# First scale as whole-fp32 products, one VectorE instruction for each other modulation unit, one square in the MLP

## The chip, the core and the metric

One core of a Trainium2 chip runs the program. The metric is the device time of one execution in microseconds (us). Its engines work side by side and wait for each other through semaphores: PE (TensorE, matrix products), DVE (VectorE), ACT (ScalarE), POOL (GpSimd) and SP, which here only issues DMAs, in the order of its queue. Each engine works through its own instructions in order.

## What is computed

Two blocks on 256 tokens of 1024 features, in fp32: eight stages in a row. The first block's two layers have a modulation that comes from one vector `c`:

```python
c_act = silu(c)
for i in range(2):
    mod = c_act @ ada_w[i] + ada_b[i]            # [1024] @ [1024, 6144]
    sh1, sc1, gt1, sh2, sc2, gt2 = split(mod, 6)
    h = rmsnorm(x, norm_g[i, 0]) * (1 + sc1) + sh1
    y = short_conv(h) if i == 0 else rwkv7(h)    # conv: h @ w_in [1024, 3072], ..., @ w_out
    x = x + gt1 * y
    h = rmsnorm(x, norm_g[i, 1]) * (1 + sc2) + sh2
    x = x + gt2 * (square(relu(h @ mlp_w1[i])) @ mlp_w2[i])   # 1024 -> 4096 -> 1024
# second block: sparse attention, MLP, decaying attention, MLP, each MLP again square(relu(.))
```

## The kernel before

Features lie on the 128 partitions (eight tiles `kt` of 128), tokens on the free axis. All large weights come as one stream of units of 128 x 1024 fp32 (512 KB; a DMA `raw` on SP brings two, 1 MB, into one of two buffers). A unit is one tile of 128 outputs against 1024 inputs. `_split` makes two fp32r parts of it: ACT copies the unit into `H` (L350) and DVE subtracts to get `L` (L352). The operand is split too (`zh`, `zl`). `mm3` then takes three products for each kt: H zh, H zl, L zh (L383 to L385), 24 products for a unit. Splits run three units ahead of the products. The stages in order, with their units: conv 32, mlp0 64, rwkv 34, mlp1 64, dsa 25, mlp2 64, fox 32, mlp3 64.

An MLP runs in two halves: 16 up units, then 16 down units (8 output tiles of two units). An up tile is evacuated as `mt` (times `rstd`, DVE L733), `mr` (relu, ACT), `hh` (square on ACT, L739), `ma` (square again on DVE, L741), `hlo` (`ma` - `hh`, DVE L744).

**The modulation.** `ada_w` has 96 units of 128 outputs x 1024 inputs, outputs on the partitions. A unit is loaded into a tile `adu` (13 buffers, SP queue; in rwkv 24 of them come as `raw`) and reduced against `cact`, a copy of silu(c) on every partition, in one of two ways: on DVE by a multiply-and-reduce (L539), or by a product on POOL (L544) followed by a summing copy on ACT (L547). The trace has 53 of the first and 43 of the second kind. Each is followed on DVE by an addition of the bias to 128 x 1 numbers (L553), and for the two scales of a layer by g (1 + scale) (L558), column by column. `ada_plan` loads a unit six stream units before it is used and multiplies on POOL two units (`PLEAD`) before the ACT sum.

**The start.** SP issues `cols`, `cact`, the input `x` in two halves, then modulation units of part (0, 0) (first scale) and (0, 1) (first shift) mixed with `raw` pairs. The squares of x are summed tile by tile on DVE into `acc`, and two products with a column of ones give the sums of a token. `conv_start` walks over kt: scale unit and shift unit of kt, then `z0` = x times rstd, `z`, `zh`, `zl`; the first six conv tiles, split in spaces of their own (`hls`, `hy`), take their products with tile kt as soon as it is there. All six finish together after kt = 7.

The order on each engine is not written by hand: a planner orders the program's instructions by priority (program order, shifted for splits and norms) and by its own costs.

The parts of the first two stages are told apart below by the start of their last evacuation: six conv tiles at 63.3 us, the 18 others at 133.4, eight output tiles at 158.1, six first mlp0 tiles at 181.3, ten more up tiles at 218.2, 16 down units at 272.4, 16 up units at 316.4, 16 down units at 361.6.

Of the kernel before, what the change touches and what calls it, by code (L numbers as in the profile page):

```python
# [29 lines left out]
PLEAD = 2  # L30
# [5 lines left out]
SHP = [1, 0, 0, 0, 0, 1, 0, 1]  # L36
# [10 lines left out]
CSL = [2, 2]  # L47
CSP = 5
CSK = [1, 2, 3, 4]
# [67 lines left out]
def rwkv_units(I):  # L117
# [4 lines left out]
    # the output product in two halves of its input, two tiles of 128 outputs in a unit  # L122
# [4 lines left out]
def rwkv_consts():  # L127
    """masks of the chunked recurrence; rows are (head of the pair, step j)"""
# [44 lines left out]
def att_consts():  # L173
    """rotary tables (rows: dims of two heads) and the causal masks"""
# [9 lines left out]
def stage_units(stage, I):  # L184
# [11 lines left out]
    if stage == "mlp2" or stage == "mlp3":  # L196
# [6 lines left out]
        ("kk", 8), ("ka", 8), ("rk", 8), ("lnw", 8), ("lnb", 8), ("gaa", 8), ("gkv", 8), ("gab", 8), ("bf", 1)]  # L203
# [7 lines left out]
# order of the modulation parts (shift, scale, gate, ...) as they are needed  # L211
# [3 lines left out]
def layout(I, stages):  # L215
# [4 lines left out]
    if len(units) % 2:  # L220
# [4 lines left out]
    ad = I["ada_w"].reshape(2, D, 6, 8, 128)[:, :, MODORD].transpose(0, 2, 3, 4, 1)  # L225
    a["ada"] = ad.reshape(48, 2, 128, D).transpose(0, 2, 1, 3)
# [9 lines left out]
        "bf": np.concatenate([I["b_f_2"], np.zeros(112, np.float32)])[:, None],  # L236
    }
# [12 lines left out]
# ---------------------------------------------------------------- the program  # L250

class Prog:
# [3 lines left out]
    def __init__(s, ctx, tc, d, out):  # L256
# [19 lines left out]
        nc.sync.dma_start(s.cols, d["cols"])  # L276
# [11 lines left out]
    def phase(s, ada, early=False):  # L288
        """the space of modulation weights"""
# [34 lines left out]
    # ---- the weight stream  # L324

    def _dma(s):
        p = s.dma_to
        s.R[p] = s.raw.tile([128, 2, D], F32, name="raw")
        n, i = s.pairs[p]
        s.nc.sync.dma_start(s.R[p], s.d[n][i])  # L330
        s.dma_to += 1

    def _split(s):
# [5 lines left out]
        if s.pairs[p][0] == "ada":  # L339
            return  # L340
# [22 lines left out]
    def ada_raw(s):  # L363
        """a unit of the stream that is a modulation's; False if a product's unit comes next"""
# [4 lines left out]
        s.ada_one(s.R[u // 2][:, u % 2], i, POOLRAW[i % len(POOLRAW)])  # L369
# [8 lines left out]
    # ---- matrix products, weights stationary  # L378
# [29 lines left out]
    def rows_gen(s, n, z, evac):  # L408
        """z (its parts) times n times 256 columns, tokens in the rows; evac(m, psums of the halves of the tokens)"""
# [34 lines left out]
    def pump(s, until):  # L444
        """issue steps of what was spawned"""
# [23 lines left out]
    def norm_shift(s, shift):  # L469
        """shift: [128, 8], a column more for the products"""  # L470
# [16 lines left out]
    def token_sums(s, ps, *accs):  # L487
        """for each accumulator, two columns of the sums over the features"""
# [27 lines left out]
    # ---- modulation of the first block  # L516

    def ada_setup(s):
# [3 lines left out]
        nc.scalar.activation(s.cact, s.cact, AF.Silu)  # L522
        s.mod = s.const.tile([128, 2, 6, 8], F32, name="mod")
# [4 lines left out]
    def ada_load(s, i):  # L528
        """unit i: (layer, part in MODORD, tile of 128 outputs)"""
# [54 lines left out]
    def conv_start(s):  # L584
        """the first norm and the first eight tiles of the convolution's products, as the modulation's weights come in"""
        nc = s.nc
        s.new_z()
        hl = [s.big.tile([128, 2, 2, KT, 128], F32R, name=f"hls{i}", tag=f"h{i}") for i in range(2)]
        hy = [s.big.tile([128, 2, KT, 128], F32R, name=f"hy{i}", tag=f"y{'hl'[i]}") for i in range(2)]
        s.hlx = dict(enumerate([hl[0][:, 0], hl[0][:, 1], hl[1][:, 0], hl[1][:, 1], hy[0], hy[1]][:GN]))  # L590
# [8 lines left out]
        for kt in range(KT):  # L599
            s.sq_feed(kt)  # L600
# [1165 lines left out]
```

## Time and profile before

| | |
|---|---|
| median of 3 runs | 1479.45 us (1477.5 to 1485.63) |
| profiled execution, span from its first to its last instruction | 1478.3 us (no time of its own around the span is given; the median lies 1.15 us above it) |
| PE busy | 1347.5 us, 91% |
| DVE busy | 1116.8 us, 76% |
| ACT busy | 774.6 us, 52% |
| POOL busy | 287.6 us, 19% |

In a list of groups each row has line, engine, operation, output <- inputs, shapes and count, then busy us, mean ns of one, and idle time before. In a timeline a row has start us, duration us, then the same names. In a table of windows a row has the stretch, its length, and for each engine the busy us and the number of instructions, then the granted PE clock (share of full), the DMA share and GB/s. Busy PE counts matmuls until their modelled end, so a stretch with waits can still read nearly full.

### The profile page before, as it was taken

How to read it: one execution, taken by the hardware profiler on the slowest of the kernel's cores; microseconds unless marked ns; L12 is line 12 of the kernel's file. 1: busy time of each engine (PE TensorE's matmuls, PEld its weight loads, DVE VectorE, ACT ScalarE, POOL GpSimd, SP SyncE). 2: the span in 40 equal slices, each digit the busy share in tenths (PEclk: the TensorE clock that was granted, in tenths of full speed). 3: DMA queues.
4: the chain of work that ended last, by engine and by line, in shares of the span. 5: the costliest groups of instructions: out<-in, count | busy, mean ns of one | idle time of the engine just before them, and what ended most of it. 6: DMA issues, size and time to landing. Idle time of an engine off the chain costs nothing.

```text
span 1478.3 us, 26839 instructions
## 1 busy us (share of the span) xinstructions
PE 1347.5 (91%) x10616; PEld 1295.6 (88%) x10616; DVE 1116.8 (76%) x2146; ACT 774.6 (52%) x1443; POOL 287.6 (19%) x224
## 2 busy tenths in 40 slices
PE   1879899998988877998999998899999999999997
PEld 1879889998778877888999987699999998999997
DVE  6889899775998998569758768877566749676665
ACT  3645574553666642226536644755355547564553
POOL 5141432102585462122000043200000000000000
PEclk9999999999889988799999999999999999999999
DMA  7577777655024553134555543246555463355553
GB/s 304 210 288 260 257 282 284 215 183 203 30 100 147 173 193 119 40 127 166 200 192 179 187 164 125 90 153 204 193 178 194 159 241 115 115 199 176 196 176 111
DMA packets 46621, 263.43 MB, mean 178 GB/s; under 512 B 5440, under 2 KB 9744, under 8 KB 20512
## 3 DMA queue, kind: packets, MB, share of 16 engines
q1 hardware_dynamic: 46288, 261.13, 50.5%
q8 instruction: 84, 1.38, 0.4%
q0 software_dynamic: 208, 0.59, 0.1%
q14 instruction: 41, 0.34, 0.1%
HBM read 257.69 MB, written 2.11 MB: 176 GB/s over the span
## 4 chain that ended last, share of the span: by engine, by line
PE 65%; DVE 21%; DMA 4%; POOL 4%; ACT 4%; issue 2%; SPq 0%; POOLq 0%; DVEq 0%; ACTq 0%
PE mm L384 18%; PE mm L383 18%; PE mm L385 18%; DVE HL L352 5%; DMA adu<-in_ada_dram 2%; DVE mod L553 2%; DVE adu L539 1%; DMA raw<-in_w_dram 1%; ACT HL L350 1%; DVE raw L539 1%; POOL adu L544 1%; PE ax L845 1%; PE mm L419 1%; PE ax L419 1%; PE ax L838 1%
## 5 line engine op out<-in xcount | busy, mean ns | idle before, releaser
L352 DVE TENSOR_TENSOR HL<-raw,HL 128x1024 fp32r<-128x1024 f32 x372 | 470.9, 1271 | 176.6 <-ACT HL L350 176.1
L350 ACT ACTIVATE HL<-raw 128x1024 fp32r<-128x1024 f32 x372 | 389.1, 1056 | 290.4 <-PE mm L385 237.2
L383 PE MATMUL mm<-zh,HL 128*128 128x256 f32 (+1 forms) x1328 | 381.9, 288 | 15.5 <-DVE mt L733 4.1
L385 PE MATMUL mm<-zh,HL 128*128 128x256 f32 (+1 forms) x1328 | 380.5, 287 | 8.8 <-DVE HL L352 8.8
L384 PE MATMUL mm<-zl,HL 128*128 128x256 f32 (+1 forms) x1328 | 379.7, 286 | 1.1 <-DVE zl L719 1.1
L384 PE MATMUL mm<-hlo,HL 128*128 128x256 f32 x1024 | 287.9, 281 | 0.0
L385 PE MATMUL mm<-hh,HL 128*128 128x256 f32 x1024 | 287.7, 281 | 0.0
L383 PE MATMUL mm<-hh,HL 128*128 128x256 f32 x1024 | 285.0, 278 | 0.0
L383 PEld LDWEIGHTS mm<-zh,HL 128*128 128x128 f32 x1328 | 255.9, 193 | 20.4 <-issue 10.5
L385 PEld LDWEIGHTS mm<-zh,HL 128*128 128x128 f32 x1328 | 256.5, 193 | 10.4 <-DVE HL L352 10.4
L384 PEld LDWEIGHTS mm<-zl,HL 128*128 128x128 f32 x1328 | 257.1, 194 | 1.4 <-DVE zl L719 1.3
L383 PEld LDWEIGHTS mm<-hh,HL 128*128 128x128 f32 x1024 | 193.3, 189 | 0.0
L384 PEld LDWEIGHTS mm<-hlo,HL 128*128 128x128 f32 x1024 | 192.5, 188 | 0.0
L385 PEld LDWEIGHTS mm<-hh,HL 128*128 128x128 f32 x1024 | 192.3, 188 | 0.0
L544 POOL TENSOR_TENSOR adu<-adu,cact 128x1024 f32<-128x1024 f32 x35 | 97.5, 2788 | 176.7 <-DMA adu<-in_ada_dram 174.6
L507 POOL TENSOR_TENSOR r<-r,mhalf 128x2 f32<-128x2 f32 x6 | 7.3, 1210 | 529.1 <-DVE r L502 529.1
L383 PE MATMUL mm<-yh,HL 128*128 128x256 f32 x272 | 81.0, 300 | 8.8 <-DVE x L1626 4.0
L384 PE MATMUL mm<-yl,HL 128*128 128x256 f32 x272 | 80.0, 295 | 0.0
L385 PE MATMUL mm<-yh,HL 128*128 128x256 f32 x272 | 79.1, 292 | 0.3 <-DVE HL L352 0.3
L741 DVE TENSOR_TENSOR ma<-mr 128x256 f32<-128x256 f32 x128 | 57.4, 455 | 17.2 <-ACT mr L736 16.6
L383 PEld LDWEIGHTS mm<-yh,HL 128*128 128x128 f32 x272 | 53.4, 198 | 10.8 <-ACT yh L1193 4.6
L736 ACT ACTIVATE mr<-mm 128x256 f32<-128x256 f32 x64 | 24.3, 383 | 69.9 <-PE mm L385 69.9
(454 smaller groups left out, 2460.5 us busy)
## 6 DMA issues: line engine op xcount, KB each, us to landing
raw<-in_w_dram SPq DMA_DIRECT2D x190, 1024.0 KB, 4.9
adu<-in_ada_dram SPq DMA_DIRECT2D x72, 512.0 KB, 7.4
raw<-in_ada_dram SPq DMA_DIRECT2D x12, 1024.0 KB, 5.1
cb<-cd SPq DMA_DIRECT2D x1, 2048.0 KB, 9.4
rs<-raw SPq DMA_DIRECT2D x28, 64.0 KB, 1.9
x<-in_x_dram SPq DMA_DIRECT2D x2, 512.0 KB, 6.7
R<-in_wa_dram SPq DMA_DIRECT2D x2, 512.0 KB, 6.8
bvd<-bv SPq DMA_DIRECT2D x8, 128.0 KB, 4.8
```

Source lines behind the costliest of these rows:

```text
L350: s.nc.scalar.activation(h, raw, AF.Copy)
L352: s.nc.vector.tensor_tensor(l, raw, h.bitcast(F32), op=OP.subtract)
L383: mm(ps, H[:, kt], rh, start=start, stop=False)
L384: mm(ps, H[:, kt], rl, start=False, stop=False)
L385: mm(ps, L[:, kt], rh, start=False, stop=stop)
L419: s.nc.tensor.matmul(ps[j][:, :256], a, b[:, k], start=kt == i == 0, stop=kt == 7 and i == 2)
L539: s.nc.vector.tensor_tensor_reduce(t, t, s.cact, scale=1.0, scalar=0.0, op0=OP.mult, op1=OP.add, accum_out=s.modf[:, i:i + 1])
L544: s.nc.gpsimd.tensor_tensor(t, t, s.cact, op=OP.mult)
L553: V.tensor_tensor(m, m, s.c("adab", i), op=OP.add)
L736: nc.scalar.activation(r, ps[:, :T], AF.Relu)
L741: nc.vector.tensor_tensor(a, r, r, op=OP.mult)
L838: tr(pt[:, 128 * j:128 * j + 128], lg[e][:, 128 * j:128 * j + 128], s.ident)
```

## The change

The first scale's eight units are stored with inputs on the partitions and multiplied on PE (eight fp32 products of one column each against `ccol`, silu(c) as columns); the result, still in PSUM, goes with the bias plus one (`a1`) into `gp` in one DVE instruction. The first six conv tiles are multiplied unsplit, in fp32: weights straight from `raw` (three pairs in spaces of their own), the operand `z` kept whole in `zf` beside its split. All other modulation units (88) are one DVE multiply-and-reduce whose starting value is the bias; POOL and ACT have no part in them, and the 128 x 1 additions are gone; g (1 + scale) is taken once for eight columns, after the eighth unit. x is loaded first on SP, in four parts, `cols` on ACT's queue; the squares of x go to PE unsummed (16 products with the column of ones in place of seven DVE additions and two). In the MLP ACT takes the square once in fp32 (`ma`) and copies it to `hh`; DVE only subtracts.

```diff
-CSL = [2, 2]
-CSP = 5
-CSK = [1, 2, 3, 4]
+ADAPE = range(8)
+CSP = 4
+CSW = [1, 3, 5]
-    def ada_one(s, t, i, pool=False):
-        if pool:
-            s.ada_mul(t)          # POOL
-            s.ada_sum(t, i)       # ACT, then ada_end on DVE
-        else:
-            s.nc.vector.tensor_tensor_reduce(t, t, s.cact, scale=1.0, scalar=0.0, op0=OP.mult, op1=OP.add,
-                                             accum_out=s.modf[:, i:i + 1])
-            s.ada_end(i)
+    def ada_one(s, t, i):
+        s.nc.vector.tensor_tensor_reduce(t, t, s.cact, scale=1.0, scalar=s.c("adab", i), op0=OP.mult, op1=OP.add,
+                                         accum_out=s.modf[:, i:i + 1])
         q, part = i % 8, i // 8 % 6
-        if part in (0, 3):
-            V.scalar_tensor_tensor(s.gpf[:, k:k + 1], m, 1.0, s.c("ng", k), op0=OP.add, op1=OP.mult)
+        if q == 7 and part in (0, 3):
+            s.nc.vector.scalar_tensor_tensor(s.gpf[:, k:k + 8], s.modf[:, i - 7:i + 1], 1.0, s.c("ng", k, 8), ...)
+    def ada_pe(s, t, ps):
+        w = t.rearrange("p (k m) -> p k m", k=KT)
+        for k in range(KT):
+            s.nc.tensor.matmul(ps, w[:, k], s.ccol[:, k:k + 1], start=k == 0, stop=k == KT - 1)
     # _split
+        if u < s.whole:
+            s.H[u], s.L[u] = s.R[p][:, u % 2].rearrange("p (k m) -> p k m", k=KT), None
+            return
     # ada_plan
-            if POOLADA[k % len(POOLADA)]:
-                at(max(u0, u - PLEAD), lambda i=i: s.ada_mul(tiles[i]))
-                at(u, lambda i=i: s.ada_sum(tiles.pop(i), i))
-            else:
-                at(u, lambda i=i: s.ada_one(tiles.pop(i), i))
+            at(u, lambda i=i: s.ada_one(tiles.pop(i), i))
     # conv_start, for each kt
+            pm = s.axbank()
+            s.ada_pe(st[kt][0], pm[:, :1])
+            s.ada_one(st[kt][1], 8 + kt)
+            loads(kt + CSP + 1)
+            V.scalar_tensor_tensor(g, pm[:, :1], a1[:, kt:kt + 1], s.c("ng", kt), op0=OP.add, op1=OP.mult)
+            V.tensor_tensor(t, s.x[:, kt], s.rstd[:, :T], op=OP.mult)
+            A.activation(z, t, AF.Identity, bias=s.mod[:, 0, 1, kt:kt + 1], scale=g)      # z = zf[:, kt]
+            A.activation(s.zh[:, kt, :T], z, AF.Copy)
+            V.tensor_tensor(s.zl[:, kt, :T], z, s.zh[:, kt, :T].bitcast(F32), op=OP.subtract)
-                    s.mm3(tiles[i][:, :T], w, k, s.zh[:, k, :T], s.zl[:, k, :T], k == 0, k == KT - 1)
+                    mm(tiles[i][:, :T], w[:, k], zf[:, k], start=k == 0, stop=k == KT - 1)
     # mlp, up
-            nc.scalar.activation(s.hh[:, m], r, AF.Square)
             a = s.t("ma")
-            nc.vector.tensor_tensor(a, r, r, op=OP.mult)
+            nc.scalar.activation(a, r, AF.Square)
+            nc.scalar.activation(s.hh[:, m], a, AF.Copy)
```

## Rows read from the trace of the kernel before

**Rows 1.** Page, part 1: the span.

```profile
span 1478.3 us, 26839 instructions
```

**Rows 2.** Windows of the start, of conv and mlp0 by part, and of rwkv's middle and end.

```profile
0.00:31.00 31.00, 3.29 (x10) 2.22 (x10) 17.85 (x29) 12.91 (x23) 16.41 (x12) 1.00 0.94 362
31.00:63.30 32.30, 23.59 (x139) 21.60 (x140) 26.27 (x49) 17.35 (x31) 6.16 (x3) 0.89 0.40 148
63.30:133.40 70.10, 60.14 (x448) 57.76 (x447) 63.22 (x109) 35.30 (x58) 26.21 (x9) 0.93 0.71 263
133.40:158.10 24.70, 23.12 (x191) 22.54 (x189) 23.83 (x43) 15.81 (x29) 2.40 (x1) 1.00 0.88 307
158.10:181.30 23.20, 19.34 (x141) 18.57 (x142) 18.95 (x33) 10.48 (x21) 12.03 (x5) 0.93 0.75 285
181.30:218.20 36.90, 32.12 (x243) 31.73 (x242) 36.38 (x65) 27.35 (x51) 10.49 (x5) 0.91 0.72 257
218.20:272.40 54.20, 51.62 (x434) 51.24 (x432) 46.14 (x67) 26.24 (x33) 17.65 (x6) 1.00 0.78 282
272.40:316.40 44.00, 43.37 (x340) 43.40 (x341) 36.29 (x65) 28.53 (x46) 0.00 (x0) 0.93 0.56 187
316.40:362.00 45.60, 45.14 (x382) 44.94 (x380) 25.39 (x34) 18.65 (x24) 0.34 (x1) 1.00 0.49 167
...
440.00:560.00 120.00, 96.95 (x758) 94.58 (x757) 110.03 (x209) 66.66 (x168) 66.47 (x50) 0.91 0.49 167
661.40:678.00 16.60, 12.60 (x94) 12.40 (x93) 15.68 (x24) 11.95 (x24) 6.52 (x3) 0.90 0.60 217
```

**Rows 3.** Timeline at 12 us: a POOL product and a DVE addition of 128 x 1.

```profile
11.85 2.62 POOL L544 TENSOR_TENSOR adu<-adu,cact 128x1024 f32<-128x1024 f32 x1 [9.90 <-DMA adu<-in_ada_dram]
12.19 2.30 DVE L553 TENSOR_TENSOR mod<-mod,cols 128x1 f32<-128x1 f32 x1
```

**Rows 4.** Groups by line and shape, whole execution.

```profile
L352 DVE TENSOR_TENSOR HL<-raw,HL 128x1024 fp32r<-128x1024 f32 x372 | 470.9, 1271 | 176.6 <-ACT HL L350 176.1
...
L544 POOL TENSOR_TENSOR adu<-adu,cact 128x1024 f32<-128x1024 f32 x35 | 97.5, 2788 | 176.7 <-DMA adu<-in_ada_dram 174.6 <-ACT yh L671 1.5
...
L741 DVE TENSOR_TENSOR ma<-mr 128x256 f32<-128x256 f32 x128 | 57.4, 455 | 17.2 <-ACT mr L736 16.6 <-ACT mr L734 0.6
...
L739 ACT ACTIVATE hh<-mr 128x256 fp32r<-128x256 f32 x128 | 52.4, 414 | 1.9
L539 DVE CUSTOM_DVE_ANT_0 adu<-adu,cact 128x1024 f32<-128x1024 f32 x37 | 47.2, 1275 | 0.0
...
L553 DVE TENSOR_TENSOR mod<-mod,cols 128x1 f32<-128x1 f32 x96 | 36.4, 396 | 4.6 <-ACT adu L547 4.1
```

**Rows 5.** Groups of DVE from 63.3 to 133.4 us.

```profile
L352 DVE TENSOR_TENSOR HL<-raw,HL 128x1024 fp32r<-128x1024 f32 x19 | 24.8, 1333 | 0.8 <-ACT HL L350 0.7
L659 DVE SCALAR_TENSOR_TENSOR cvv<-u,cols,cvv 128x256 f32<-128x256 f32 x16 | 13.8, 868 | 0.7 <-ACT cvv L655 0.6
...
L553 DVE TENSOR_TENSOR mod<-mod,cols 128x1 f32<-128x1 f32 x17 | 8.4, 511 | 0.0
```

**Rows 6.** Timeline of PE: fp32 products of 256, of one and of two columns.

```profile
378.51 0.60 PE L1215 MATMUL ax<-hx,R 128*128 128x256 f32 x2
378.95 0.60 PE L1216 MATMUL ax<-hx,R 128*128 128x256 f32 x2
...
15.41 1.01 PE L491 MATMUL ax<-ones,acc 128*128 128x1 f32 x4 [15.41 <-DVE acc L778]
...
449.68 0.51 PE L1367 MATMUL ax<-rc,R 128*128 128x2 f32 x4
```

**Rows 7.** SP's timeline: issues of the third pair and of the last first-shift units.

```profile
35.99 0.33 SPq L330 DMA_DIRECT2D raw<-in_w_dram  x1
36.37 0.90 SPq L531 DMA_DIRECT2D adu<-in_ada_dram  x2
```

**Rows 8.** Chain that ended last, in order of time: one piece of mlp0.

```profile
231.20 5.64 DMA adu<-in_ada_dram
```

More of the change, by code (lines that the diff above doesn't have):

```diff
@@ L225, in layout @@
     ad = I["ada_w"].reshape(2, D, 6, 8, 128)[:, :, MODORD].transpose(0, 2, 3, 4, 1)
+    ad = ad.reshape(96, 128, D).copy()
+    for i in ADAPE:
+        ad[i] = ad[i].T.reshape(KT, 128, 128).transpose(1, 0, 2).reshape(128, D)
     a["ada"] = ad.reshape(48, 2, 128, D).transpose(0, 2, 1, 3)
@@ L236, in layout @@
         "bf": np.concatenate([I["b_f_2"], np.zeros(112, np.float32)])[:, None],
+        "cc": col(I["c"].reshape(-1)),
     }
@@ L275, in __init__ @@
         s.cols = s.const.tile([128, NCOL], F32, name="cols")
-        nc.sync.dma_start(s.cols, d["cols"])
+        nc.scalar.dma_start(s.cols, d["cols"])
         s.ident = s.const.tile([128, 128], F32, name="ident")
@@ L327, in _dma @@
         p = s.dma_to
-        s.R[p] = s.raw.tile([128, 2, D], F32, name="raw")
+        s.R[p] = s.rawx.pop(p) if p in s.rawx else s.raw.tile([128, 2, D], F32, name="raw")
         n, i = s.pairs[p]
@@ L500, in _norm_close, with _norm_factor @@
         s.token_sums(ps, s.acc)
+        return s._norm_factor(ps, squared, copy)
+    def _norm_factor(s, ps, squared=False, copy=True):
+        nc = s.nc
         r = s.wk.tile([128, 2], F32, name="r")
@@ L522, in ada_setup @@
         nc.scalar.activation(s.cact, s.cact, AF.Silu)
+        s.ccol = s.const.tile([128, KT], F32, name="ccol")
+        nc.scalar.activation(s.ccol, s.c("cc"), AF.Silu)
         s.mod = s.const.tile([128, 2, 6, 8], F32, name="mod")
@@ L586, in conv_start @@
         nc = s.nc
+        V, A, mm = nc.vector, nc.scalar, nc.tensor.matmul
         s.new_z()
-        hl = [s.big.tile([128, 2, 2, KT, 128], F32R, name=f"hls{i}", tag=f"h{i}") for i in range(2)]
-        hy = [s.big.tile([128, 2, KT, 128], F32R, name=f"hy{i}", tag=f"y{'hl'[i]}") for i in range(2)]
-        s.hlx = dict(enumerate([hl[0][:, 0], hl[0][:, 1], hl[1][:, 0], hl[1][:, 1], hy[0], hy[1]][:GN]))
+        hs = [s.big.tile([128, 2, 2, D], F32, name=f"hs{i}", tag=f"h{i}") for i in range(2)]
+        s.rawx = {p: hs[p // 2][:, p % 2] for p in range((GN + 1) // 2)}
+        s.whole = GN
+        sq = s.big.tile([128, KT, T], F32, name="sq0", tag="yh")
+        zf = s.big.tile([128, KT, T], F32, name="zf", tag="yl")
         st = []
@@ L596, in loads @@
                 st.append((s.ada_load(kt), s.ada_load(8 + kt)))
-        for i in (0, 4):
-            nc.sync.dma_start(s.x[:, i:i + 4], s.d["x"][:, i:i + 4])
-        for kt in range(KT):
-            s.sq_feed(kt)
-        s.norm_close()
-        for n in CSL:
-            loads(n)
-            s._dma()
-        loads(CSP)
-        tiles, units, at = [], [], []
-        for kt in range(KT + 1):
-            if kt < KT:
-                s.ada_mul(st[kt][1])
-                s.ada_one(st[kt][0], kt)
-            if kt:
-                j = kt - 1
-                s.ada_sum(st[j][1], 8 + j)
-                t = s.t("z0")
-                nc.vector.tensor_tensor(t, s.x[:, j], s.rstd[:, :T], op=OP.mult)
-                z = s.t("z1")
-                nc.scalar.activation(z, t, AF.Identity, bias=s.mod[:, 0, 1, j:j + 1], scale=s.gp[:, 0, j:j + 1])
-                nc.scalar.activation(s.zh[:, j, :T], z, AF.Copy)
-                nc.vector.tensor_tensor(s.zl[:, j, :T], z, s.zh[:, j, :T].bitcast(F32), op=OP.subtract)
-            loads(kt + CSP)
-            while len(units) < GN and kt >= CSK[len(units) // 2]:
-                units.append(s.unit(0))
-                tiles.append(s.mmbank() if len(tiles) < 3 else s.axbank())
@@ new lines, in loads @@
+                if kt in CSW:
+                    s._dma()
+        loads(CSP)
+        a1 = s.wk.tile([128, KT], F32, name="a1")
+        V.tensor_scalar(a1, s.c("adab", 0, KT), 1.0, None, op0=OP.add)
+        for kt in range(KT):
+            A.activation(sq[:, kt], s.x[:, kt], AF.Square)
+        ps = s.axbank()
+        for j in range(2):
+            for kt in range(KT):
+                mm(ps[:, j:j + 1], sq[:, kt, 128 * j:128 * j + 128], s.ones, start=kt == 0, stop=kt == KT - 1)
+        s._norm_factor(ps)
@@ new lines, in conv_start @@
+        tiles = [s.mmbank() if i < 3 else s.axbank() for i in range(GN)]
+        units, at = [], []
+        for kt in range(KT):
+            pm = s.axbank()
+            s.ada_pe(st[kt][0], pm[:, :1])
+            s.ada_one(st[kt][1], 8 + kt)
+            loads(kt + CSP + 1)
+            g = s.gp[:, 0, kt:kt + 1]
+            V.scalar_tensor_tensor(g, pm[:, :1], a1[:, kt:kt + 1], s.c("ng", kt), op0=OP.add, op1=OP.mult)
+            t = s.t("z0")
+            V.tensor_tensor(t, s.x[:, kt], s.rstd[:, :T], op=OP.mult)
+            z = zf[:, kt]
+            A.activation(z, t, AF.Identity, bias=s.mod[:, 0, 1, kt:kt + 1], scale=g)
+            A.activation(s.zh[:, kt, :T], z, AF.Copy)
+            V.tensor_tensor(s.zl[:, kt, :T], z, s.zh[:, kt, :T].bitcast(F32), op=OP.subtract)
+            while len(units) < GN and kt >= CSW[len(units) // 2]:
+                units.append(s.unit(0)[0])
@@ L624, in conv_start @@
                 at.append(0)
             for i, w in enumerate(units):
-                while at[i] < kt:
+                while at[i] <= kt:
                     k = at[i]
-                    s.mm3(tiles[i][:, :T], w, k, s.zh[:, k, :T], s.zl[:, k, :T], k == 0, k == KT - 1)
+                    mm(tiles[i][:, :T], w[:, k], zf[:, k], start=k == 0, stop=k == KT - 1)
                     at[i] += 1
@@ L1633, in run @@
         s.feed = lambda kt: None
-        s.hlx = {}
+        s.hlx, s.rawx, s.whole = {}, {}, 0
         s.early = next((s.start[n] for n in stages if n not in ("conv", "mlp0")), 2 * len(s.pairs))
         s.phase(ADAB if first else 0, True)
-        if stages[0] != "conv":
-            nc.scalar.dma_start(s.x, s.d["x"])
+        for i in range(0, KT, 2):
+            nc.sync.dma_start(s.x[:, i:i + 2], s.d["x"][:, i:i + 2])
         if first:
```

23 lines of the change are left out of this document (6 added, 17 removed).

## Prediction

> **What bounds the kernel now.** I read the table of windows first, cut where a part of a stage ends [rows 2]. A part whose products are never late shows PE's own pace: the last 16 units of mlp0 take 45.6 us, 2.85 us a unit, 0.119 us for each of its 24 products. The reader then holds every other part of the first two stages against that pace. The 18 conv units from 63.3 to 133.4 us need 51.3 and take 70.1 (18.8 lost); the eight of the output product need 22.8 and take 24.7 (1.9); the six first of mlp0 17.1 against 23.2 (6.1); the next ten 28.5 against 36.9 (8.4); the 16 down units 45.6 against 54.2 (8.6); the two parts after 272.4 lose nothing. So some 44 us are lost between 63.3 and 272.4, and before 63.3 us only six tiles are finished. What ends the waits is in the DVE column of the same rows: 63.2 of 70.1, 23.8 of 24.7, 36.4 of 36.9. DVE sets the pace there; in the down part (46.1 of 54.2) something else does.
>
> Why DVE is so full shows the timeline beside it [rows 3]: a DVE addition of 128 numbers of one column starts 0.34 us after a POOL product and ends with it, 2.30 us later. The same addition takes 0.396 on the mean over all 96 [rows 4]. DVE stands while POOL multiplies. In the conv part the lines on DVE are long in the same way [rows 5]: L659 868 ns, L553 511 ns, L352 1333 ns.
>
> The down part has its own cause. The chain of waits there holds the landing of a modulation unit, 5.64 us after its issue [rows 8], with the POOL product, the ACT sum and so ACT's next splits behind it; SP issues such a unit only behind a `raw` pair that waits for its buffer. The start shows the same queue [rows 7]: the third pair is issued at 35.99 us, when a first split frees its buffer, and the last two units of the first scale and shift stand behind it until 36.37, with DMA idle ahead (148 GB/s from 31 to 63.3, 362 before [rows 2]).
>
> **The change, part by part.** All sums are against the span of 1478.3 us [rows 1]; the median shown is 1.15 us above it.
>
> *Start.* The bytes up to the last first-shift unit: 16 modulation units of 0.524 MB, three pairs of 1.05, x 1.05, `cact` 0.52, `cols` 0.16, together 13.3 MB. The kernel before moved 362 x 31 = 11.2 MB in its first 31 us; at that mean rate the other 2.1 take 5.8 us, so the last unit lands near 37. No issue waits for a buffer any more: the pairs have their own space, and the 13 buffers of units are reused only after a first product. PE's work: 64 one-column products and 48 whole products. One column costs (1.01 / 4) 0.25 us in the start's rows and 0.51 / 4 = 0.13 us later [rows 6], which I take as PE's clock at its lower and its higher level. A whole product of 256 columns costs (378.95 - 378.51) / 2 = 0.22 us [rows 6], less than the three split ones, 0.36. At the lower level I double it. So PE needs 8 + 11 = 19 us at the higher and 16 + 21 = 37 at the lower level, from about 17 us (token sums at 15.41 now [rows 6]). At the higher level data sets the end: 37 plus eight one-column products (1), four small dependent steps on DVE and ACT (2, at some 0.45 each [rows 4]), six whole products (1.3): 41. At the lower, with the chain gp, z, product unhidden (0.6 us for each kt): 59. The stretch that holds the head now had a clock of 0.89 [rows 2], so I take 46, nearer to the higher level: 17 us earlier than 63.3 (4 to 22). The 16 products of squares (4 us at most) replace a sum that DVE took tile by tile; same answer either way. Six splits (1.27 us each [rows 4]) leave DVE and ACT; their gain is inside this term.
>
> *Conv, 18 units.* DVE gains what POOL's nine products [rows 2] held. Against quiet durations (1.215 for L352, 0.48 for L659, 0.15 for L553) the three lines of rows 5 are long by 2.2 + 6.2 + 6.1 = 14.5 us, 1.6 for each POOL product (at most 2.15, as in rows 3). The additions' own 17 x 0.15 = 2.6 and the eight gp columns (1.2) go too. It takes on nine reductions at 1.275 [rows 4] less overlap, 1.2: 10.8. The sum is -7.5, to 62.6 us, still above PE's 51.3. I take -8 (-4, if ACT's and DMA's waits grow; -14 if every POOL product had cost 2.15 and lines outside rows 5 shrink).
>
> *Output product and first six mlp0 tiles.* Losses 1.9 and 6.1. One and four POOL products fall away, but the second shift's eight reductions are in DVE's order just before its products, and the first norm_split waits for g (1 + scale) of all eight columns. I take -3 (0 to -6).
>
> *Next ten up tiles.* 16 times `ma` leave DVE (0.455 each, 7.3 us [rows 4]), and four or five POOL products' waits (7), for five reductions (6). DVE falls from 36.4 to about 28, PE's own 28.5. I take -7 (-4 to -8.4).
>
> *Down units.* A unit is now needed only at its own time instead of two units (5.7 us) earlier, which is what the landing missed [rows 8], and ACT's queue no longer holds a sum. But SP's order stays, and DVE, not POOL, now stands if a unit is late, and behind it the splits. I take -6 (-3 to -8.6).
>
> *rwkv.* 440 to 560 has DVE at 110 of 120 us [rows 2] and the inverse of the triangles on it. Six to eight POOL products (1.6 each, 11) and 24 additions (0.1 to 0.15 without POOL, 3) go, eight reductions (10) come: -4 on a full engine, and ACT and POOL are freer: I take -6 (+2 to -10).
>
> *End of rwkv, mlp1.* 661.4 to 678 is four units (11.4) in 16.6 us with DVE at 15.7 and three POOL products: -2.5 (0 to -5).
>
> *The square elsewhere.* From 272.4 on PE sets the pace of the MLPs [rows 2], so the DVE time of the other 112 `ma` (51 us) is cover, not gain: nothing. ACT takes 0.41 more for each tile [rows 4]: from 28.5 us in the 44 of an up part to 35, still covered by PE. That cover is gone only if a tile's ACT work passes 2.75 us.
>
> *Starting value.* A bias column in place of the constant 0.0 in the reduction shows nowhere. Nothing to some 0.07 us (L659's quiet 0.48 against 0.41 of a two-input form) for 88, at most 6 us, partly hidden; I take nothing.
>
> Sum: 17 + 8 + 3 + 7 + 6 + 6 + 2.5 = 49.5 us; 1478.3 - 49.5 = 1428.8, and with 1.15 for the median, 1430.
>
> *A rule against it.* The rows give a whole fp32 product as 0.22 us [rows 6], two split ones. The Trainium skill, FP8 and Floating Point Precision, TensorE Precision Notes, counts four passes through the array for true FP32. By it 48 whole products would take some 23 us at the higher level instead of 11. The trace disagrees, with its 0.22 beside it; it is a rival below.
>
> **Rivals.**
> DVE stays the bound: 35 more reductions land on an engine with 63 of 70 us busy, and DMA bursts keep waits as they are. Then only the start, half of the up part and 1 or 2 elsewhere remain, some 22 us: 1457. For it: DVE needs 62 us where PE needs 51; against it: rows 3. Chance 0.15.
> The start runs at the lower clock: 59 instead of 46, 1443. For it: 64 products of one column in a thin stream, 0.25 us each at 15 us; against it: the products between them. Chance 0.12.
> Whole products cost as much again in this place, 0.44 at the higher level, if the pair that rows 6 time is no measure of 48: 48 x 0.22 = 10.6 us of PE work more, all of it on the start's end: 1440. Against it, each of the rows' two pairs gives 0.22. Chance 0.03. (This is where the rule of the Trainium skill's FP8 and Floating Point Precision would lead.)
> All that was lost comes back, PE bound from 42 us on: 21 + 18 + 8 + 8 + 8 + 10 = 73: 1406. Chance 0.09.
> The change does not free DVE: if its long instructions were long for another reason, it gains 17 + 5 and pays 25 reductions of 1.2 less the additions in the same parts: 1473 to 1483. Rows 3 say otherwise. Chance 0.03.
> Slower: ACT becomes the bound of the up parts. The copy waits for the square just ahead of it, and if that pair cost not 0.41 but 1.5 us more for a tile, the 112 tiles that PE bounds now would each lose (28.5 / 16 + 1.5 - 2.75 =) 0.53 us, 60 us in all, more than the 49.5: 1490. For it: two dependent instructions in a row; against it: 414 ns on the mean [rows 4]. Chance 0.03.
>
> **How the numbers follow.** The forecast, 1430, has 0.55 (its own range 1414 to 1446). The range 1408 to 1458 takes in the clock and the pass rivals, most of a bound DVE, and the sum's ends for all but extreme mixes. Faster by over 0.5%, about 7.4 us and what a measurement of this kernel can tell from no change: 0.55 + 0.15 + 0.12 + 0.03 + 0.09 = 0.94; within: 0.03; slower: 0.03.
>
> **What would show it.** In the windows of the changed kernel: six conv tiles done near 46 us, with DMA above 360 GB/s until 37; POOL without L544 and no DVE line above its quiet time; whole products 0.22 us apart; 18 conv units in about 62 us with DVE still full; ten up tiles near 30; down units near 48; 44 to 46 as now for the late halves of the MLPs. Wrong would be a start beyond 55 us, a conv part still at 70, or a late MLP half above 47 with ACT full.

## The result, and the profile after

The changed kernel takes 1439.14 us (median of 4 runs, 1434.7 to 1442.18) beside 1480.7 for the kernel before (4 runs in the same comparison): ratio 0.971, 95% interval 0.968 to 0.974. That is 41.6 us less, inside the range and 9 us above the forecast of 1430. The sum hides two large errors, though. The table sets the parts beside the forecast; a part ends at the start of its last evacuation, but the start and the six mlp0 tiles, which finish together, at the first (the start 62.2 us before), all from the timelines of the two profiled executions, which differ by 39.3 us at the last part's end.

| part | before | after | measured | forecast |
|---|---|---|---|---|
| start, six conv tiles | 62.2 | 62.4 | +0.2 | -17 |
| 18 conv units | 71.1 | 58.3 | -12.8 | -8 |
| output product, first six mlp0 tiles | 46.5 | 43.7 | -2.8 | -3 |
| ten up tiles | 38.6 | 34.6 | -4.0 | -7 |
| 16 down units | 54.0 | 46.2 | -7.8 | -6 |
| late half of mlp0 | 89.2 | 88.6 | -0.6 | 0 |
| rwkv | 316.2 | 303.0 | -13.2 | -6 and most of -2.5 |
| mlp1 to the end | 790.6 | 792.3 | +1.7 | rest of -2.5 |

The windows of the changed kernel, cut at these ends, answer to [rows 2]: stretch, its length, busy us and number of instructions of PE, PEld, DVE, ACT and POOL, the granted PE clock, DMA share and GB/s.

```profile
0.00:31.00 31.00, 22.57 (x108) 21.09 (x109) 8.48 (x28) 8.54 (x18) 1.61 (x6) 1.00 0.95 364
31.00:62.40 31.40, 30.48 (x143) 25.55 (x142) 10.45 (x22) 6.97 (x12) 0.00 (x0) 0.78 0.41 167
62.40:120.70 58.30, 56.02 (x452) 54.54 (x451) 55.07 (x101) 26.81 (x42) 0.00 (x0) 1.00 0.84 306
120.70:146.20 25.50, 22.78 (x193) 22.61 (x192) 23.66 (x43) 13.69 (x26) 0.00 (x0) 1.00 0.90 309
146.20:164.40 18.20, 16.40 (x131) 15.57 (x130) 16.06 (x30) 7.84 (x14) 1.68 (x1) 1.00 0.86 319
164.40:199.00 34.60, 33.35 (x277) 32.97 (x276) 32.66 (x57) 29.57 (x57) 0.00 (x0) 1.00 0.82 303
199.00:245.20 46.20, 46.09 (x389) 45.89 (x389) 40.23 (x56) 19.44 (x21) 0.00 (x0) 1.00 0.88 314
245.20:288.50 43.30, 43.30 (x363) 43.30 (x362) 32.48 (x49) 34.26 (x61) 0.00 (x0) 1.00 0.58 196
```

From 62.4 us on this is the picture that was forecast: POOL empty, DVE still full in the conv part (55.1 of 58.3), the down units near PE's own pace, the late up half unchanged with ACT at 34.3 of 43.3. The second row is not. From 31 to 62.4 us DVE is busy for a third and ACT for less, the transfers are over by 45 us, and PE is busy for 30.5 of 31.4 us. The groups of PE between 5 and 63.4 us say with what.

```profile
L630 PE MATMUL mm<-zf,hs 128*128 128x256 f32 x48 | 18.9, 549 | 2.9 <-ACT zf L621 2.7
L558 PE MATMUL ax<-ccol,adu 128*128 128x1 f32 x128 | 18.1, 275 | 0.0
L630 PE MATMUL ax<-zf,hs 128*128 128x256 f32 x44 | 11.9, 421 | 0.0
L607 PE MATMUL ax<-ones,sq 128*128 128x1 f32 x32 | 7.0, 353 | 5.5 <-ACT sq L603 5.5
```

The counts are what the reader is to see. The code issues 64 one-column products (L558) and 16 of squares (L607); the trace has 128 and 32. Six tiles of 8 whole products are 48; the trace has 48 in the `mm` banks alone and as many in the `ax` banks (44 of them by 63.4 us). One fp32 product is two instructions. What the prediction took from [rows 6] as two products 0.22 us apart was one product. How PE goes through them is in its timeline (start, duration, then the names):

```profile
13.99 6.83 PE L558 MATMUL ax<-ccol,adu 128*128 128x1 f32 x32
...
23.96 2.93 PE L630 MATMUL mm<-zf,hs 128*128 128x256 f32 x6 [1.86 <-ACT zf L621]
26.68 4.01 PE L558 MATMUL ax<-ccol,adu 128*128 128x1 f32 x32
30.55 1.74 PE L630 MATMUL mm<-zf,hs 128*128 128x256 f32 x4
33.17 5.08 PE L630 MATMUL mm<-zf,hs 128*128 128x256 f32 x12 [0.88 <-ACT zf L621]
38.09 1.89 PE L630 MATMUL ax<-zf,hs 128*128 128x256 f32 x8
39.82 3.63 PE L558 MATMUL ax<-ccol,adu 128*128 128x1 f32 x32
...
48.31 5.78 PE L630 MATMUL ax<-zf,hs 128*128 128x256 f32 x26
53.92 3.63 PE L558 MATMUL ax<-ccol,adu 128*128 128x1 f32 x32
57.41 2.16 PE L630 MATMUL mm<-zf,hs 128*128 128x256 f32 x6
```

From 26.68 us on each group starts where the one ahead ends, but for one wait of 0.88 us for `zf`: two scale units (x32), then the whole products that these two kt allow, then the next two scale units. From 53.92 to 57.41 us, 32 instructions of one column take 3.49 us, 0.109 each; from 48.31 to 53.92, 26 of 256 columns take 5.61, 0.216 each. Both stretches have a clock of 1.00, the level of 2.4 GHz. So a scale unit costs PE 16 x 0.109 = 1.7 us there, and a whole product 0.43, more than the three split ones it replaces (0.36).

Earlier the same work takes twice as long: 6.83 / 32 = 0.213 us for one column from 13.99 us on, (26.68 - 23.96) / 6 = 0.45 for 256 columns. That is the spacing of the lower level, 1.2 GHz, as in this window, whose column reads 0.50 (in the timeline its products stand 0.43 us apart):

```profile
33.00:36.00 3.00, 2.83 (x7) 2.26 (x8) 1.63 (x3) 0.54 (x2) 0.00 (x0) 0.50 1.04 415
```

The column reads 1.00 for the first 31 us all the same. Up to some 27 us here, and for longer in some of the kernels below, the spacing and the column disagree, and the level is read from the spacing.

The groups of DVE from 62.4 to 120.7 us answer to [rows 5]:

```profile
L356 DVE TENSOR_TENSOR HL<-raw,HL 128x1024 fp32r<-128x1024 f32 x19 | 22.8, 1227 | 0.3 <-ACT HL L354 0.3
L545 DVE CUSTOM_DVE_ANT_0 adu<-adu,cact,cols 128x1024 f32<-128x1024 f32 x16 | 20.2, 1287 | 0.0
L661 DVE SCALAR_TENSOR_TENSOR cvv<-u,cols,cvv 128x256 f32<-128x256 f32 x16 | 7.7, 487 | 0.6 <-ACT cvv L657 0.5
```

The split fell from 1333 to 1227 ns and L659 (now L661) from 868 to 487: in the kernel below that only takes POOL out they are at 1234 (whole execution) and 480, so POOL's part made them long.

### The profile page after: what moved, and what is told of

Its sections match the earlier page's. It is cut to its first block, busy times and chain, and to the rows that moved or that the text cites. A ratio compares the mean times of both kernels' runs of the same rounds, so it can differ in the third digit from the quotient of the medians.

```text
span 1439.8 us, 26749 instructions
## 1 busy us (share of the span) xinstructions
PE 1357.8 (94%) x10724; PEld 1303.4 (91%) x10724; DVE 1019.3 (71%) x1959; ACT 772.5 (54%) x1480; POOL 172.8 (12%) x181
## 4 chain that ended last, share of the span: by engine, by line
PE 72%; DVE 15%; DMA 4%; POOL 4%; ACT 2%; issue 2%; POOLq 0%; DVEq 0%; SPq 0%; ACTq 0%
PE mm L388 18%; PE mm L387 18%; PE mm L389 18%; DVE HL L356 4%; DMA raw<-in_w_dram 3%; DVE adu L545 2%; PE mm L630 1%; PE ax L558 1%; PE mm L423 1%; PE ax L423 1%; PE ax L847 1%; ACT HL L354 1%; PE ax L630 1%; PE ax L840 1%; POOL R L1455 1%
## 5 line engine op out<-in xcount | busy, mean ns | idle before, releaser
L356 DVE TENSOR_TENSOR HL<-raw,HL 128x1024 fp32r<-128x1024 f32 x372 | 458.1, 1238 | 229.5 <-ACT HL L354 229.0
L389 PE MATMUL mm<-zh,HL 128*128 128x256 f32 (+1 forms) x1328 | 376.1, 284 | 5.9 <-DVE HL L356 5.8
L387 PE MATMUL mm<-zh,HL 128*128 128x256 f32 (+1 forms) x1328 | 376.8, 284 | 4.4 <-DVE x L701 1.6
L388 PE MATMUL mm<-zl,HL 128*128 128x256 f32 (+1 forms) x1328 | 375.1, 283 | 0.0
L387 PEld LDWEIGHTS mm<-zh,HL 128*128 128x128 f32 x1328 | 251.3, 189 | 8.4 <-issue 3.8
L389 PEld LDWEIGHTS mm<-zh,HL 128*128 128x128 f32 x1328 | 251.5, 190 | 7.6 <-DVE HL L356 7.6
L388 PEld LDWEIGHTS mm<-zl,HL 128*128 128x128 f32 x1328 | 252.2, 190 | 0.0
L545 DVE CUSTOM_DVE_ANT_0 adu<-adu,cact,cols 128x1024 f32<-128x1024 f32 x64 | 81.2, 1280 | 2.0 <-DMA adu<-in_ada_dram 2.0
L746 DVE TENSOR_TENSOR hlo<-ma,hh 128x256 fp32r<-128x256 f32 x128 | 53.5, 421 | 5.8 <-ACT hh L743 3.1
L743 ACT ACTIVATE hh<-ma 128x256 fp32r<-128x256 f32 x128 | 52.9, 417 | 3.5
```

Of the source, the lines that this page charges most:

```text
L356: s.nc.vector.tensor_tensor(l, raw, h.bitcast(F32), op=OP.subtract)
L387: mm(ps, H[:, kt], rh, start=start, stop=False)
L388: mm(ps, H[:, kt], rl, start=False, stop=False)
L389: mm(ps, L[:, kt], rh, start=False, stop=stop)
L743: nc.scalar.activation(s.hh[:, m], a, AF.Copy)
L746: nc.vector.tensor_tensor(s.hlo[:, m], a, s.hh[:, m].bitcast(F32), op=OP.subtract)
```

## The experiments

Eleven kernels ran, in three comparisons, each with runs of the kernel before. It took 1479.55 us beside POOL taken out, the scale on DVE and the two with split products; 1480.27 beside the unread products, the squares of x and the two on the MLP square; 1481.33 beside the half scale, the three tiles and the small additions.

**POOL taken out of the kernel before, nothing else.** All 96 units on DVE, in the long form with an addition of their own.

```diff
-            if POOLADA[k % len(POOLADA)]:
+            if False:
...
-                s.ada_mul(st[kt][1])
                 s.ada_one(st[kt][0], kt)
+                s.ada_one(st[kt][1], 8 + kt)
...
-                s.ada_sum(st[j][1], 8 + j)
```

> The kernel before with one edit: every modulation unit is reduced on DVE, none on POOL and ACT; the additions of 128 x 1, the start's order and its split tiles, and the two squares stay. Theory (DVE stands while POOL multiplies): the gains behind the start come from this edit alone but for the square's and the additions' share: conv's 18 units 71 to 60 us, rwkv 10 us less, the whole at 1442 to 1455. Rival (DVE stays the bound, since 43 more reductions of 1.3 us land on it): 1470 or more.

Measured: 1428.15 us, ratio 0.965 (0.961 to 0.969). This edit alone gives 51 us, more than the whole change. First tile at 52.2 us (62.2 before), 18 conv units in 56.5, down units in 45.6, rwkv in 304.5. The theory's mechanism holds; its range (1442 to 1455) is missed by 14 us, 10 of them in the start, which it had left alone. And DVE, which took over 43 reductions, is busy for less than before, as part 1 of the page says:

```profile
PE 1327.7 (93%) x10616; PEld 1278.6 (90%) x10616; DVE 1084.6 (76%) x2232; ACT 728.6 (51%) x1357; POOL 176.2 (12%) x181
```

1084.6 us against 1116.8 in the kernel before. What follows: POOL did not help DVE, it cost DVE more than it took off it. The rest of the change, taken together, loses some 10 us of this.

**The POOL products back, but with nobody waiting for them.** To the last kernel, behind each reduction that POOL had shared in: a product of the same size whose result is not read.

```diff
+        if pool:
+            s.nc.gpsimd.tensor_tensor(t, t, s.cact, op=OP.mult)
...
```

> The kernel before with every modulation unit reduced on DVE (the last run, -52 us), and behind each reduction that stood on POOL in the kernel before one POOL product of the same size again, whose result nobody reads: 43 products, none of which anything waits for except the buffer that is loaded next. Theory: a POOL product holds DVE while both work on SBUF, by 1.6 us or more each where DVE sets the pace; then most of the 52 us are lost again: 20 to 45 us above 1428, so 1448 to 1473, and lines on DVE become long again (the one-column addition above 0.3 us on the mean). Rival: what the POOL units cost was their place in the queues (the sum on ACT, the unit needed two units earlier); an unread product then costs 0 to 6 us: 1426 to 1434.

Measured: 1506.07 us, ratio 1.016 (1.013 to 1.018), 25.8 us above the kernel before where the last one lay 51.4 below it: 77 us, 1.8 for each of the 43 products. The theory's mechanism holds and its size was too small; the rival is out. Four groups of DVE, first of this kernel, then of the one without POOL products:

```profile
L352 DVE TENSOR_TENSOR HL<-raw,HL 128x1024 fp32r<-128x1024 f32 x372 | 480.9, 1297 | 165.3 <-ACT HL L350 164.7
L535 DVE CUSTOM_DVE_ANT_0 adu<-adu,cact 128x1024 f32<-128x1024 f32 x72 | 93.0, 1306 | 0.0
L551 DVE TENSOR_TENSOR mod<-mod,cols 128x1 f32<-128x1 f32 x96 | 44.0, 470 | 0.0
...
L556 DVE SCALAR_TENSOR_TENSOR gp<-mod,cols 128x1 f32<-128x1 f32 x32 | 24.2, 760 | 0.0
```

```profile
L352 DVE TENSOR_TENSOR HL<-raw,HL 128x1024 fp32r<-128x1024 f32 x372 | 457.5, 1234 | 173.0 <-ACT HL L350 170.7 <-PE mm L385 2.0
L536 DVE CUSTOM_DVE_ANT_0 adu<-adu,cact 128x1024 f32<-128x1024 f32 x72 | 86.5, 1218 | 0.3 <-DMA adu<-in_ada_dram 0.3
...
L550 DVE TENSOR_TENSOR mod<-mod,cols 128x1 f32<-128x1 f32 x96 | 15.7, 174 | 0.0
...
L555 DVE SCALAR_TENSOR_TENSOR gp<-mod,cols 128x1 f32<-128x1 f32 x32 | 6.8, 217 | 0.0
```

The four are longer by 23.4 + 6.5 + 28.3 + 17.4 = 75.6 us, of 88.5 that DVE's busy time grew in all (1084.6 to 1173.1). That this is near the 77 us of the whole is in part chance, since DVE does not set the pace everywhere. By parts the time grew by 17.8 us in the 18 conv units (56.5 to 74.3), 15.9 in the down units (45.6 to 61.5), 14.2 in rwkv (304.5 to 318.7), 10.8 in the output product and the up tiles between them, and 16.5 in the start (52.2 to 68.7), where PE's clock was lower too (0.64 from 31 us to its end, 0.77 without the products). SP also waits 29.3 us, in six places, for POOL to be done with a `raw` buffer; no run separates that from what POOL does to DVE. One case, in the timelines of POOL and of DVE of the kernel with the products:

```profile
75.16 2.59 POOL L539 TENSOR_TENSOR adu<-adu,cact 128x1024 f32<-128x1024 f32 x1 [10.30 <-DVE u L648]
```

```profile
75.00 0.49 DVE L656 SCALAR_TENSOR_TENSOR cvv<-u,cols,cvv 128x256 f32<-128x256 f32 x1
...
75.40 2.37 DVE L551 TENSOR_TENSOR mod<-mod,cols 128x1 f32<-128x1 f32 x1
77.69 0.47 DVE L656 SCALAR_TENSOR_TENSOR cvv<-u,cols,cvv 128x256 f32<-128x256 f32 x1
```

The DVE instruction that had begun runs on; the next one, 128 numbers with two inputs in SBUF, ends when POOL ends (75.16 + 2.59 = 77.75; 75.40 + 2.37 = 77.77). The Trainium skill, SBUF — State Buffer, Who interferes with whom, says that a DVE instruction with two SBUF inputs and a GpSimd instruction that reads SBUF shut each other out, the second waiting until the first is done; the rows agree.

**The first scale back on DVE, in the changed kernel.**

```diff
-            s.ada_pe(st[kt][0], pm[:, :1])
+            s.ada_one(st[kt][0], kt)
...
```

> The changed kernel with the first scale's eight units reduced on DVE as all others are; the six conv tiles stay whole. Theory (PE's work sets the end of the start, because each fp32 product is two instructions): PE loses the 128 one-column instructions, 18.1 us in the changed kernel's groups, DVE takes 8 more of 1.36 us in a stretch where it is busy a third of the time. The six tiles end at 45 to 49 us in place of 63.4, the whole at 1422 to 1427. Rival (the start is long because its products run at the lower clock, and a thinner stream lowers it further): six tiles not before 58 us, the whole within 5 us of 1439.

Measured: 1420.95 us, ratio 0.962 (0.958 to 0.966); first tile at 46.7 us. The theory holds, with the time 1 us below its range: the eight units on PE cost 18 us, 15.7 of them in the start. PE's timeline there:

```profile
33.14 1.89 PE L627 MATMUL ax<-zf,hs 128*128 128x256 f32 x8
34.87 1.46 PE L627 MATMUL mm<-zf,hs 128*128 128x256 f32 x6
36.16 0.59 PE L627 MATMUL ax<-zf,hs 128*128 128x256 f32 x2
36.59 1.46 PE L627 MATMUL mm<-zf,hs 128*128 128x256 f32 x6
37.89 5.78 PE L627 MATMUL ax<-zf,hs 128*128 128x256 f32 x26
```

Whole products alone, 0.216 us an instruction again (1.29 for six, 5.61 for 26). From 31 us on PE bounds this start too (busy for 15.70 of 15.70 us), but with less to do. With the run on the squares of x below, this is the fastest kernel of the study.

**Half of the scale units on PE.** The first four there, the last four on DVE.

> The changed kernel with the first four units of the first scale on PE and the last four reduced on DVE. Theory: each unit on PE costs the bound engine its 16 instructions (0.275 us each on the mean, 4.4 us a pair of units) and keeps its clock low; half of them gives back half of the 18 us that all eight cost, or more, since the later four lie where PE waits for nothing: first tile at 48 to 55, 1425 to 1432. Rival: the loss is that the products with one column stand between whole products at all, so half of them cost as much: 60 us and 1437 to 1440.

Measured: 1429.52 us, ratio 0.967 (0.964 to 0.969); first tile at 54.0. Both lie in the theory's ranges. Against the last kernel four units cost 7.3 us of the start, 1.8 each; the other four cost 8.4 more. So the loss goes by the unit, but not at one price:

```profile
13.87 6.83 PE L558 MATMUL ax<-ccol,adu 128*128 128x1 f32 x32
...
26.57 6.83 PE L558 MATMUL ax<-ccol,adu 128*128 128x1 f32 x32
```

The four take 13.7 us of PE here, at the lower level's 0.213 for an instruction. About half of that shows, since PE has idle time there: in the last kernel it waits 8.5 us for `zf` before 31 us. The other four stand at 39.82 and 53.92 us in the changed kernel, at 0.109, 7.0 us in all, and show in full. That the units keep the clock low, as the theory has it, is not separated from their price.

**Three whole tiles instead of six.**

```diff
-GN = 6
+GN = 3
-CSW = [1, 3, 5]
+CSW = [1, 3]
```

> The changed kernel with three conv tiles instead of six made of whole fp32 products in the start; the other three are made later from split parts. Theory: PE's own work bounds the start (57 of 58 us busy, a whole product 0.43 to 0.86 us), so 24 whole products less shorten it by 10 to 15 us (first tile done at 47 to 52), and 21 conv tiles instead of 18 take 8 to 10 us more: 1432 to 1438. Rival: the data or the chain from the last modulation unit bounds the start; then it ends at 58 to 62 us as before and the three tiles are pure loss: 1445 to 1449.

Measured: 1439.46 us, ratio 0.972 (0.970 to 0.974); first tile at 60.6, 21 conv units in 63.4. The start lies in the rival's range, the time in neither: data does not bound the start (no transfer is left at 45 us), and the three tiles are no loss. Half of the whole products are gone and the start is only 1.8 us shorter. The windows of 3 us of this kernel show why:

```profile
39.00:42.00 3.00, 3.00 (x24) 2.83 (x23) 0.00 (x0) 0.00 (x0) 0.00 (x0) 1.00 0.63 255
42.00:45.00 3.00, 3.00 (x17) 3.00 (x17) 1.50 (x4) 1.02 (x2) 0.00 (x0) 0.57 0.04 18
45.00:48.00 3.00, 3.00 (x10) 2.46 (x10) 1.67 (x4) 1.02 (x2) 0.00 (x0) 0.50 0.00 0
48.00:51.00 3.00, 3.00 (x15) 3.00 (x15) 0.11 (x1) 0.00 (x0) 0.00 (x0) 0.50 0.00 0
51.00:54.00 3.00, 3.00 (x10) 2.46 (x9) 1.64 (x4) 1.02 (x2) 0.00 (x0) 0.50 0.00 0
54.00:57.00 3.00, 3.00 (x15) 3.00 (x15) 0.14 (x2) 0.00 (x0) 0.00 (x0) 0.50 0.00 0
57.00:60.60 3.60, 3.60 (x9) 2.62 (x9) 2.04 (x5) 1.05 (x3) 0.00 (x0) 0.50 0.00 0
```

From 45 us on PE has the lower level, 1.2 GHz, through to the end of the start, busy for the whole of each stretch and with all data there; up to 39.05 us it had that level's spacing too (32 one-column instructions from 26.64 us stand 0.21 apart), so only some 3 us of this start ran at the higher one. In the changed kernel the same stretches read 0.51 at 45, 1.00 from 48 to 57 and 0.70 after it. Less work was done at half the speed. So PE bounds the start, but its pace depends on the clock too, and the theory had priced the instructions alone. Why the clock stayed low with half of the whole products gone is open.

**Split products in the start, with the scale on PE and with it on DVE.** The six tiles as three fp32r products each, from split weights.

```diff
-                    mm(tiles[i][:, :T], w[:, k], zf[:, k], start=k == 0, stop=k == KT - 1)
+                    s.mm3(tiles[i][:, :T], w, k, s.zh[:, k, :T], s.zl[:, k, :T], k == 0, k == KT - 1)
...
```

> The changed kernel with the first six conv tiles split and multiplied as three fp32r products again, the first scale still on PE. Theory (a whole product costs 0.43 us at the higher clock, more than three split ones at 0.36): PE's part for the six tiles falls from 31.7 us to 17 to 25, six splits of 1.25 us come back to DVE and ACT, which have room; six tiles end at 54 to 60 us, the whole at 1430 to 1438. Rival (the whole products pay, because a split and its wait cost more than PE's passes): six tiles at 66 us or later, the whole at 1443 or more.

> Both edits: first scale on DVE, six tiles split, POOL still out of it. Theory: PE has 7 us of squares and 17 of products before the end, so the landing of the last units (37 to 39 us) and DVE behind it (16 reductions, six splits, eight small steps, some 40 us from 10 us on) set it: six tiles at 45 to 52 us, the whole at 1420 to 1430. Rival (the whole products are what makes an all-DVE start possible): six tiles at 58 us or later, the whole above 1436.

Measured: 1442.04 us (0.975, 0.972 to 0.978) with the scale on PE, first tile at 67.2; 1424.64 (0.964, 0.961 to 0.967) with it on DVE, first tile at 52.8. The first theory is missed in both numbers; of its rival the start holds (66 or later) and the time is 1 us short. The second theory's time holds, its start is missed by 0.8 us. Whole products end the start 5 to 6 us earlier than split ones in both pairs (62.4 and 46.7), although they take more of PE. A group of PE before 53 us, in the kernel with the scale on DVE, shows part of the reason:

```profile
L387 PE MATMUL mm<-zh,hy 128*128 128x256 f32 x8 | 3.6, 452 | 9.8 <-ACT hy L354 7.4 <-ACT zh L618 2.2
```

Split weights wait for ACT (7.4 us of PE's idle time); unsplit ones are ready when they land. Ahead of the start's products PE is idle for 14.6 us here and for 8.5 with whole ones. The split ones also keep the lower level's spacing up to some 37 us, the whole ones up to 32 with a short rise before; how much of the 6 us that makes is not shown. In the times of the whole kernels the gain is 3 to 4 us, with overlapping intervals.

**The squares of x summed on DVE as well.** On top of the scale on DVE: seven additions in place of the 16 products.

> The changed kernel with the first scale's eight units on DVE (the run at 1420.95) and the squares of x summed on DVE too instead of by 16 products with one column on PE. Theory: the squares end before the modulation weights have landed either way, so six conv tiles are done at 45 to 48 us and the time is 1418 to 1424. Rival: the eight additions on DVE delay the reductions behind them, which now are on the chain in the first 29 us: 3 to 5 us later, 1423 to 1427.

Measured: 1420.63 us (0.960, 0.957 to 0.963), first tile at 46.0: the same as 1420.95. The theory holds. The 7.0 us that the 16 products (L605 there) take of PE cost nothing in that kernel; with the scale on PE it was not tried.

**The square taken once in the kernel before, and twice in the changed one.**

```diff
-            nc.vector.tensor_tensor(a, r, r, op=OP.mult)
-            nc.scalar.activation(s.hh[:, m], r, AF.Square)
+            nc.scalar.activation(a, r, AF.Square)
+            nc.scalar.activation(s.hh[:, m], a, AF.Copy)
```

> The kernel before with the MLP square taken once (ACT squares, ACT copies the rounded part; DVE loses 128 multiplications), nothing else. Theory: the square's DVE time matters only in the first MLP's upper part, where DVE is full (38.6 us): 16 x 0.46 = 7 us leave it, and 2 to 7 of them show, so 1473 to 1478; everything later is unchanged. Rival: it shows nowhere, since the dependent pair on ACT takes its place as the last to be ready: 1478 to 1483.

> The changed kernel with the square taken twice again (DVE multiplies, ACT squares), nothing else. Theory: with POOL gone DVE has room for it, as the upper part of the run without POOL shows (32.2 us with the square twice, 34.6 in the changed kernel with it once): the part stays at 32 to 36 us and the time at 1436 to 1442. Rival: the 16 multiplications of 0.46 us come back on a DVE that is busy for 32.7 of 34.6 us: 3 to 7 us more, 1442 to 1447.

Measured: 1478.96 us in the kernel before (ratio 1.000, 0.998 to 1.002), 1440.59 in the changed one (0.973, 0.970 to 0.976, against its 0.971): no difference of the whole in either. The rival of the first and the theory of the second hold. Within the first the parts moved: the ten up tiles took 46.1 us (38.6 in the kernel before, ACT busy for 36.8) and the down units 49.3 (54.0). The window of the ten up tiles with the square twice and no POOL:

```profile
163.60:197.70 34.10, 32.04 (x266) 31.67 (x265) 33.38 (x67) 22.89 (x40) 0.00 (x0) 1.00 0.87 317
```

34.1 us against 34.6 with it once: 16 multiplications back on DVE raise its busy time by 0.7 us there and ACT falls from 29.6 to 22.9. What the change took from DVE it gave to ACT; here, without POOL, the part's length moved by 0.5 us.

**The small additions back.** The changed kernel with starting value 0.0, the bias addition of its own and g (1 + scale) column by column.

> The changed kernel with the bias added by an instruction of its own again behind each reduction, and g times 1 + scale computed column by column: 88 additions and 24 such products more on DVE, of 0.17 and 0.22 us each as the run without POOL has them, 20 us in all. Theory: they show only where DVE sets the pace (18 conv units with some 14 of them, and the recurrent mixer with 48): 2 to 7 us, 1441 to 1446. Rival: most lie in idle time of DVE: 0 to 2 us, 1437 to 1441.

Measured: 1446.49 us (0.975, 0.972 to 0.978), but with runs from 1436.7 to 1448.77, and the interval overlaps that of the changed kernel. The theory's size fits and its place does not (56 of the 88 additions lie ahead of the end of mlp0 and 24 in rwkv, where it had 48): to the end of mlp0 both stand at the same time (333.7 and 333.8 us), rwkv takes 304.9 against 303.0, and the rest of the difference lies behind rwkv, in parts that hold only eight of the additions (1.2 us). By the parts the additions are worth 2 us at most, within the scatter of rwkv (see below); the other 5 stay open. The groups show that the edit is not free on either side:

```profile
L546 DVE CUSTOM_DVE_ANT_0 adu<-adu,cact 128x1024 f32<-128x1024 f32 x64 | 77.4, 1218 | 0.4 <-DMA adu<-in_ada_dram 0.4
...
L548 DVE TENSOR_TENSOR mod<-mod,cols 128x1 f32<-128x1 f32 x88 | 14.9, 177 | 0.2
```

```profile
L545 DVE CUSTOM_DVE_ANT_0 adu<-adu,cact,cols 128x1024 f32<-128x1024 f32 x64 | 81.2, 1280 | 2.0 <-DMA adu<-in_ada_dram 2.0
```

The starting value from a column (second fence, the changed kernel) makes each reduction 0.06 us longer and saves an addition of 0.18.

## Why the prediction was right, and where it was wrong

*Start, -17, measured 0: the failed step.* "A whole product of 256 columns costs (378.95 - 378.51) / 2 = 0.22 us": the x2 of [rows 6] is one product of two instructions, and the same holds for one column (0.13 and 0.25 are 0.22 and 0.43). Data does not set the end here; PE does. With measured prices its work is 128 x 0.109 + 96 x 0.216 = 34.7 us at the higher level and twice that at the lower, where the prediction had 19 and 37. PE took from 13.99 to 63 us for it, between the two: some 27 of these 49 us were at the lower level (up to 27 us by the spacing, then by the column, 0.78 on the mean from 31 us on). The 0.89 [rows 2] that made it take 46, near the higher level, misled it: in the kernel before, too, the products up to 39.8 us stand 0.21 apart (0.12 later) while the column reads 1.00 (31 to 40 us). Its own sign of being wrong, a start beyond 55 us, came. The same trace holds the correction: the code issues 8 products at L1215 and 16 are recorded. The runs with the scale on DVE put the price in the start at 15.7 us, and the run with half of it shows that it goes by the unit. The rule of the Trainium skill that the prediction set aside (FP8 and Floating Point Precision, TensorE Precision Notes: four passes for true FP32) was nearer: 0.43 us is 3.6 times the 0.119 of one fp32r product [rows 2].

*The rivals of the start.* "Whole products cost as much again", held at 0.03, came true, and for one-column products too, which it had left out; that its 1440 lies 1 us from the measured time is luck, since the parts behind the start gave 7 us more than it counts. "The start runs at the lower clock" came true in part, for some 27 of 49 us.

*Conv, -8, measured -12.8.* Right mechanism, a low price: where the sum took 1.6 us for a POOL product, the unread products cost this part 17.8 us for eight, 2.2 each, and the column of gp counts with it (760 ns against 217 in the whole execution).

*Output product and first mlp0 tiles (-3, measured -2.8), down units (-6, measured -7.8)*: as forecast. The down part lost POOL's hold on DVE, the ACT sum and the early need together. The unread products alone stretch it from 45.6 to 61.5 us, so POOL's products would be enough to explain it; what the other two had in it is open.

*Ten up tiles, -7, measured -4.* The term counted 7.3 us of `ma` as leaving DVE; the two runs on the square show no gain from that (in the kernel before the part even grew). POOL taken out alone gives 6.4 us here (38.6 to 32.2), and the rest of the change takes 2.4 of it back.

*rwkv, -6 and most of -2.5, measured -13.2.* Mis-sized: POOL alone gives 11.7 there (316.2 to 304.5 in the first experiment). The part took 295.3 to 303.1 us in eight kernels with the same instructions in it, so what the reductions' short form adds can't be read from it.

*Late halves, squares elsewhere, ACT as the bound: 0, as forecast* (43.3 and 45.3 us). "DVE stays the bound" failed for the conv part only in degree: DVE is still busy for 55.1 of 58.3 us.

So the forecast was near by luck, by two errors of opposite sign: 17 us that did not come in the start, and some 8 more than expected where POOL had been. The four steps that can be told apart add up, from 1479.55 to 1439.14: POOL out -51.4 (1479.55 to 1428.15), small ends, loads and square -3.5 (to 1424.64), whole products -3.7 (to 1420.95), first scale on PE +18.2 (to 1439.14). The two in the middle are within the intervals; the others are shown. (The last step and the others come from two comparisons, whose kernel before differs by 1 us.)

## What to carry to other kernels

Before work is moved to an engine, count the instructions that one product leaves in the trace against those that the code issues; here a row's x2 was one product, and the price of everything on PE doubled. Work on POOL that reads SBUF was not free for DVE: 43 products there cost 77 us, while 43 reductions on DVE take 43 x 1.218 = 52 us of it, so check whether DVE lines are long while POOL runs before sharing work with it. In a start that waits for data, the engine that has the products should get no second job with one column at a time; an idle DVE took it for 18 us less.

## What was not expected of the hardware

Moving 43 reductions from POOL to DVE lowered DVE's busy time, from 1116.8 to 1084.6 us. A start with half of the whole products ran at the lower clock for all but some 3 us and took almost as long (60.6 against 62.4 us), with PE busy throughout from 45 us on in both. And a product with one column in fp32 costs two instructions of 0.109 us at the higher level, half of what two with 256 columns cost. The profile's column of the granted clock read 1.00 over the first 27 us of the changed kernel, while its products stood as far apart as at 0.50.
